# Gate/up products of a decoder trunk: sevens for half of the steps in every second group, and leftovers ordered by priority

## The chip, the core and the metric

The kernel runs on one core of a Trainium2 chip, in one launch. The metric is the device time of an execution in microseconds. Five engines matter: PE (TensorE: matrix products, and its separate weight load PEld), DVE (VectorE), ACT (ScalarE), POOL (GpSimd, almost unused) and SP, whose queue issues the transfers (DMA).

## What is computed

Two layers over 256 tokens of width 2048, all in float32. Layer 0 mixes tokens by causal trailing means, layer 1 by differential attention with eight heads; each is followed by a dense SwiGLU block with 5632 hidden columns. The last step is a normalisation.

```python
for i in range(DEPTH):                       # 2 layers
    hn = rmsnorm(h, norm_mix[i])
    mix = pool_mixer(hn, ...) if i % 2 == 0 else diff_attention(hn, ...)
    h = h + mix
    h = h + swiglu(rmsnorm(h, norm_ffn[i]), w_gate[i], w_up[i], w_down[i])
return rmsnorm(h, final_norm)

def swiglu(h, wg, wu, wd):
    return (jax.nn.silu(h @ wg) * (h @ wu)) @ wd
```

## The kernel before

**Products in two halves.** A float32 operand is split into a high part (`hi`, rounded to the matrix engine's faster float32r type, a cast on ACT) and the rest (`lo`, a subtraction on DVE). A product of two blocks is then three products on PE: high by high, high by low, low by high. Each has 128 x 128 stationary values (activations) and 512 moving columns (weights).

**Groups and steps.** `group()` computes one output of 256 tokens x 1024 columns as 2 x 2 blocks: two blocks of tokens, two blocks of 512 columns. It walks over the contraction in steps of 256 rows; a step takes 1 MB of weights, four blocks of 128 x 512, as one transfer `raw` (`load`). Gate/up has 11 groups a layer (512 gate and 512 up columns each), each of 8 steps. Down has two groups (`o`) for each chunk of the hidden columns; `CHUNKS` says that a chunk is 4, 4 and 3 gate/up groups, so a down group has 8, 8 or 6 steps. The attention layer has four groups for q and k, two for v and two for the output projection, 8 steps each.

**A plain step** makes `whi` and `wlo` of all four blocks (`halves`: 2048 columns on ACT, 2048 on DVE) and issues 4 x 2 x 3 = 24 products into the four PSUM banks C11, C12, C21, C22.

**A step by sevens** computes the same 2 x 2 product of blocks with seven block products in place of eight (the Strassen-Winograd scheme), 7 x 3 = 21 products on PE, into seven banks M1, M2, M6, M7, P5, P3, P4. For that DVE makes four sums of weight blocks (`sums`: one instruction of 1024 columns at L121, two of 512 at L123 and L124), ACT and DVE split these (`thi` at L130, `tlo` at L131, 2048 columns each), and of the raw blocks only three need splitting (1536 columns). The activation pairs of such a step are held in an eight-block form, made once for each pair by `pair()`. Which steps go by sevens is given by `SEVEN` for gate/up, `SEVEN_DOWN`, `SEVEN_QKV` and `SEVEN_O`. With both kinds of step in one group, C11, C12 and C21 share the banks of M2, P3 and P4 (6, 4 and 5), and C22 has bank 7, called X.

**The end of a group.** `combined()` adds the seven results and X into four tiles c11, c12, c21, c22: two copies on ACT, then eight instructions of 512 columns on DVE (L202 to L211). A gate/up group goes on with silu on ACT (L463), a product on DVE (L464), and two calls of `pair()`, which transpose the hidden values on PE into PSUM (L250, a bank of `aux`, which takes banks 0 to 3 in turn), and split them (L254 and L255, or by way of the tile `e`, L263 to L268, where the down step will go by sevens). A down group adds its result to the residual `x_tok` (L487).

**Buffers.** `raw`, `whi` and `wlo` have three buffers each, `tsum`, `thi` and `tlo` one each, the tiles of the combination one each, and each of the eight PSUM banks is a buffer by itself.

**What sets the order.** No order is written out by hand. A scheduler runs through the program at compile time with estimated durations: of the instructions of an engine whose operands and buffers are ready, it takes the one of highest priority, which is the one that stands earliest in the program. The order that it finds is fixed for each engine's queue; on the chip, semaphores hold an instruction until what it needs is done. `tc.high_priority(-n)` moves an instruction's priority back by n places.

Of the kernel before, what the change touches and what calls it, by code (L numbers as in the profile page):

```python
# [38 lines left out]

SEVEN = (2, 4, 6)  # L40
SEVEN_DOWN = (2, 4, 6)
SEVEN_QKV = (4, 6)
SEVEN_O = (6,)


# [7 lines left out]
def trunk_kernel(ctx, tc, x_n, gains, scale_in, final_in, subln, lam_in, band, dist,  # L53
# [18 lines left out]

    turn = {"aux": 0, "of": 4}

    def bank(i, shape=(P, 512)):
        return psum.tile(list(shape), F32, name=f"b{i}", tag=f"b{i}")


# [5 lines left out]
    gain_sb = const.tile([P, 6, NK], F32, name="gain_sb")  # L84
    dist_sb = const.tile([P, 2 * P], F32, name="dist_sb")
    ident = const.tile([P, P], F32, name="ident")
    ones = const.tile([P, P], F32, name="ones")
    nc.vector.memset(ones, 1.0)
    make_identity(nc, ident)

    x_tok = resid.tile([P, 2, D], F32, name="x_tok")
# [8 lines left out]
    def tile_of(xp, k):  # L100
        return xp[k // 2][:, k % 2]

    def f32(ap):
        return ap.bitcast(F32)
# [33 lines left out]
    def group(steps, pool, by_bank=0):  # L138
# [14 lines left out]
        ps = {}  # L153

# [8 lines left out]
        def products(a, seven, w, b, parts):  # L163
            first = b not in ps
            if first:
                ps[b] = bank(b)
            for at, which, block in parts:
                hi, lo = w[which]
                if seven:
                    ah, al = a[:, 0, at], a[:, 1, at]  # L170
                else:
                    k, t = at
                    if a.shape[2] == 8:
                        slot = ((A11, A21), (A12, A22))[k][t]
                        ah, al = a[:, 0, slot], a[:, 1, slot]
                    else:
                        ah, al = (a[:, k, i, t * P:(t + 1) * P] for i in range(2))
                for x, y in ((ah, hi), (ah, lo), (al, hi)):
                    left[b] -= 1
                    nc.tensor.matmul(ps[b], x, y[:, block], start=first, stop=(left[b] == 0))  # L180
                    first = False
# [13 lines left out]
    def combined(ps, pool):  # L195


        if M1 not in ps:
            return [[ps[C11], ps[C12]], [ps[C21], ps[C22]]]
        m1, u2, u3, p5 = (pool.tile([P, 512], F32, name=f"c{i}") for i in ("11", "12", "21", "22"))  # L200
        nc.scalar.copy(m1, ps[M1])
        nc.vector.tensor_tensor(u2, ps[M6], m1, ALU.add)  # L202
        nc.vector.tensor_tensor(m1, ps[M2], m1, ALU.add)  # L203
        nc.vector.tensor_tensor(u3, ps[M7], u2, ALU.add)
        nc.scalar.copy(p5, ps[P5])
        nc.vector.tensor_tensor(u2, p5, u2, ALU.subtract)
        nc.vector.tensor_tensor(p5, p5, u3, ALU.subtract)
        nc.vector.tensor_tensor(u2, ps[P3], u2, ALU.add)
        nc.vector.tensor_tensor(u3, ps[P4], u3, ALU.add)
# [34 lines left out]

    def pair(dst, src, gains, seven):

        ps = aux((P, 2, 2, P))
        for i in range(2):
# [12 lines left out]

        for i, at in ((0, slice(A21, A11 + 1)), (1, slice(A22, A12 + 1, A12 - A22))):
            nc.scalar.activation(e[:, at], ps[:, i], AF.Copy, scale=1.0 if gains is None else gains[i])  # L263
        nc.vector.tensor_tensor(e[:, S1:S3 + 1], e[:, A21:A11 + 1], e[:, A22:A21 + 1], ALU.subtract)
        nc.vector.tensor_tensor(e[:, S2], e[:, S1], e[:, A11], ALU.subtract)
        nc.vector.tensor_tensor(e[:, S4], e[:, A12], e[:, S2], ALU.add)
        nc.scalar.copy(dst[:, 0], e)
        nc.vector.tensor_tensor(dst[:, 1], e, f32(dst[:, 0]), ALU.subtract)  # L268

# [10 lines left out]
    with tc.tile_pool(name="start", bufs=1, reuse_waits="tile") as st:  # L280

        warm = tmp.tile([P, 8], F32, name="warm", bufs=1)
        nc.scalar.activation(warm[:, 0:1], ones[:, 0:1], AF.Sqrt)
        wp = aux()
# [47 lines left out]
        def product(g, some):  # L332

            if some[0] == 0:
                yp[g] = [bank(4 + 2 * (g % 2) + t) for t in range(2)]
                if g >= PLAIN:
# [76 lines left out]
    turn["of"] = 4  # L413
    nc.sync.dma_start(out=dist_sb, in_=dist)

    def finish(cs, ys, final_sb, ss):

        for t in range(2):
            part = tmp.tile([P, 64], F32, name="part", bufs=2)
            nc.vector.tensor_reduce(part[:, 0:1], ss[:, t, 0:2], AX.X, ALU.add)  # L420
# [22 lines left out]
    def ffn(layer, xq, ss, next_op, next_gain):  # L443
# [3 lines left out]
        with tc.tile_pool(name=f"ffn{layer}", bufs=1, reuse_waits="tile") as hp:  # L447
            g0 = 0
            ys = []
            for c, n in enumerate(CHUNKS):  # L450
# [6 lines left out]
                for g in range(g0, g0 + n):  # L457

                    by_seven = SEVEN[-1:] if g == 0 and layer == 0 else SEVEN
                    cs = combined(group([(xq[p], p in by_seven, w_gu[layer][g, p]) for p in range(NP)], hp), hp)  # L460
# [4 lines left out]
                    for i in range(2):  # L465
                        at = 2 * (g - g0) + i
                        ht = hp.tile(pair_shape(at in SEVEN_DOWN), F32R, name="h", tag=f"h{at}")
                        pair(ht, lambda k, t: cs[t][1][:, (2 * i + k) * P:(2 * i + k + 1) * P], None, at in SEVEN_DOWN)
                        hp_tiles.append(ht)
                for o in range(2):  # L470
# [35 lines left out]
    with tc.tile_pool(name="attn", bufs=1, reuse_waits="tile") as ap_, ExitStack() as heads:  # L506
# [3 lines left out]
        qs_col, subln_sb, lam_sb, lp, le, neg_lam, gs = (  # L510
            small[:, a:b] for a, b in ((0, 2), (2, 4), (4, 8), (8, 10), (10, 12), (12, 13), (14, 16)))
        nc.sync.dma_start(out=subln_sb, in_=subln)
        nc.sync.dma_start(out=lam_sb, in_=lam_in)
        r_col = row_scale(ss)
        nc.vector.tensor_scalar(qs_col, r_col, QK_SCALE, None, ALU.mult)

        nc.vector.tensor_tensor(lp, lam_sb[:, 0:2], lam_sb[:, 2:4], ALU.mult)
        l_ps = aux()
# [74 lines left out]
        for g in range(2):  # L593
            cs = scaled(combined(group([(xp[p], p in SEVEN_QKV, w_v[g, p]) for p in range(NP)], op_), op_), (r_col, r_col))
            for h in range(4 * g, 4 * g + 4):
# [11 lines left out]
                for t in range(2):  # L607
                    nc.scalar.activation(on[:, t, :], op[:, t, :], AF.Copy, scale=ro[:, t:t + 1])
                oT[h] = op_.tile(pair_shape(h in SEVEN_O), F32R, name=f"oT{h}")
                pair(oT[h], lambda i, t: on[:, t, i * P:(i + 1) * P], [gs[:, i:i + 1] for i in range(2)], h in SEVEN_O)  # L610
# [98 lines left out]
```

## Time and profile before

| | |
|---|---|
| median of 3 runs (lowest to highest) | 1845.67 us (1845.63 to 1845.7) |
| the profiled execution: time, span of its instructions | 1846.21 us, 1844.4 us |
| PE, weight load, DVE, ACT: busy share of the span | 99%, 81%, 87%, 56% |
| HBM read | 353.36 MB, 193 GB/s over the span |

How to read the rows that follow. An instruction's row gives its start in the span, its duration (both in us), engine, line of the kernel and operation, `out<-in` by the kernel's names, shapes, and a count where several were merged; in square brackets stand the idle time of its engine ahead of it and what ended that. A row of the waits is: who waited, for whom, microseconds in all, times, longest. A row of busy time by stretch gives the stretch, its length, the busy time of PE, PEld, DVE, ACT and POOL with instruction counts, then the granted clock, the DMA share and GB/s. PE's products overlap, so a product's row is longer than its distance to the next.

### The profile page before, as it was taken

To read this page: it belongs to the slowest core of one execution; us is meant where nothing else is said; L and a number is where in the kernel's file an instruction comes from. 1 tells how busy PE (TensorE), PEld (TensorE's weight loads), DVE (VectorE), ACT (ScalarE), POOL (GpSimd) and SP (SyncE) were. 2 spreads that over 40 slices of the span, in tenths; PEclk is the share of its full clock that TensorE was granted. 3 is DMA by queue.
4 is the path that set the end of the run, shared out by engine and by line. 5 is a ranking of instruction groups with operands and counts; after the bars stand their busy time and mean duration, and the time that the engine had idled before them with its cause. 6 is when DMAs were issued, how large, how long until landed. Compare 5 with 4: busy or idle time off the path is not lost.

```text
span 1844.4 us, 20901 instructions
## 1 busy us (share of the span) xinstructions
PE 1829.2 (99%) x8210; PEld 1495.6 (81%) x8210; DVE 1604.2 (87%) x1662; ACT 1038.0 (56%) x1006; POOL 0.7 (0%) x6
## 2 busy tenths in 40 slices
PE   9999999999999999999999999999999999999998
PEld 6788888888888888888888888788888888888886
DVE  6889998898989899988888678998989899998986
ACT  6555555555554556665566655555555555545553
POOL 0000000000000000000000000000000000000000
PEclk9999999999999999999999999999999999999999
DMA  7555555655555555555454454555555555565552
GB/s 273 183 201 187 193 210 194 210 196 194 203 198 204 202 186 183 208 180 171 173 177 164 160 188 176 205 203 187 204 205 204 188 201 183 206 227 204 206 186 111
DMA packets 50642, 356.80 MB, mean 193 GB/s; under 512 B 6000, under 2 KB 6128, under 8 KB 8048
## 3 DMA queue, kind: packets, MB, share of 16 engines
q1 hardware_dynamic: 49824, 353.85, 54.4%
q10 hardware_dynamic: 720, 1.62, 0.2%
q8 instruction: 64, 1.05, 0.2%
q14 instruction: 34, 0.28, 0.0%
HBM read 353.36 MB, written 2.10 MB: 193 GB/s over the span
## 4 chain that ended last, share of the span: by engine, by line
PE 95%; DVE 2%; ACT 1%; issue 1%; DMA 1%; SPq 0%; DVEq 0%; ACTq 0%
PE b L180 90%; PE b L250 2%; PE b L342 1%; DVE wlo L116 1%; PE b L554 1%; PE b L345 1%; PE b L584 0%; DMA w<-pool_w 0%; DMA raw<-w_gu 0%; DVE tlo L131 0%; ACT whi L115 0%; DVE tsum L121 0%; PE b L600 0%; PE b L598 0%; PE b L599 0%
## 5 line engine op out<-in xcount | busy, mean ns | idle before, releaser
L115 ACT CAST whi<-raw 128x1536 fp32r<-128x1536 f32 (+1 forms) x330 | 585.2, 1774 | 585.4 <-PE b L180 499.6
L180 PE MATMUL b<-whi,xp 128*128 128x512 f32 x2824 | 908.8, 392 | 1.2 <-DVE c L203 1.0
L116 DVE TENSOR_TENSOR wlo<-raw,whi 128x1536 fp32r<-128x1536 f32 (+1 forms) x330 | 697.3, 2113 | 193.1 <-ACT whi L115 192.9
L180 PEld LDWEIGHTS b<-whi,xp 128*128 128x128 f32 x2824 | 528.3, 188 | 110.1 <-DVE c L203 1.5
L180 PE MATMUL b<-wlo,xp 128*128 128x512 f32 x1412 | 551.8, 391 | 1.6 <-DVE wlo L116 1.6
L180 PE MATMUL b<-whi,h 128*128 128x512 f32 x1108 | 354.5, 390 | 0.0
L180 PEld LDWEIGHTS b<-wlo,xp 128*128 128x128 f32 x1412 | 265.3, 188 | 55.5 <-DVE wlo L116 1.9
L131 DVE TENSOR_TENSOR tlo<-tsum,thi 128x2048 fp32r<-128x2048 f32 x108 | 246.7, 2285 | 3.9 <-ACT thi L130 3.9
L180 PEld LDWEIGHTS b<-whi,h 128*128 128x128 f32 x1108 | 207.5, 188 | 43.1
L180 PE MATMUL b<-wlo,h 128*128 128x512 f32 x554 | 215.8, 389 | 0.0
L130 ACT CAST thi<-tsum 128x2048 fp32r<-128x2048 f32 x108 | 206.3, 1910 | 13.7 <-DVE tsum L124 13.6
L180 PE MATMUL b<-thi,xp 128*128 128x512 f32 x608 | 211.8, 390 | 0.0
L121 DVE TENSOR_TENSOR tsum<-raw 128x1024 f32<-128x1024 f32 x108 | 131.8, 1220 | 2.3 <-DMA raw<-w_v 0.6
L180 PEld LDWEIGHTS b<-thi,xp 128*128 128x128 f32 x608 | 113.9, 188 | 24.0 <-ACT thi L130 0.9
L180 PEld LDWEIGHTS b<-wlo,h 128*128 128x128 f32 x554 | 104.0, 188 | 21.3
L180 PE MATMUL b<-tlo,xp 128*128 128x512 f32 x304 | 119.5, 393 | 0.0
L180 PE MATMUL b<-thi,h 128*128 128x512 f32 x240 | 83.7, 389 | 0.0
L124 DVE TENSOR_TENSOR tsum<-tsum,raw 128x512 f32<-128x512 f32 x108 | 74.3, 688 | 2.3
L123 DVE TENSOR_TENSOR tsum<-tsum,raw 128x512 f32<-128x512 f32 x108 | 73.9, 684 | 0.6
L180 PE MATMUL b<-whi,oT 128*128 128x512 f32 x236 | 74.4, 392 | 0.0
L180 PEld LDWEIGHTS b<-tlo,xp 128*128 128x128 f32 x304 | 57.0, 188 | 16.1 <-DVE tlo L131 4.4
L180 PEld LDWEIGHTS b<-thi,h 128*128 128x128 f32 x240 | 45.1, 188 | 9.2
(147 smaller groups left out, 1192.5 us busy)
## 6 DMA issues: line engine op xcount, KB each, us to landing
raw<-w_gu SPq DMA_DIRECT2D x176, 1024.0 KB, 4.9
raw<-w_down SPq DMA_DIRECT2D x88, 1024.0 KB, 4.8
raw<-w_qk SPq DMA_DIRECT2D x32, 1024.0 KB, 4.9
raw<-w_v SPq DMA_DIRECT2D x16, 1024.0 KB, 4.8
raw<-w_o SPq DMA_DIRECT2D x16, 1024.0 KB, 4.8
raw<-pool_w SPq DMA_DIRECT2D x2, 1024.0 KB, 13.8
x_tok<-x_n SPq DMA_DIRECT2D x2, 768.0 KB, 9.0
w<-pool_w SPq DMA_DIRECT2D x2, 512.0 KB, 6.6
```

The source lines that it names most:

```text
L115: nc.scalar.copy(hi[:, lo_block:], raw[:, lo_block:])
L116: nc.vector.tensor_tensor(lo[:, lo_block:], raw[:, lo_block:], f32(hi[:, lo_block:]), ALU.subtract)
L121: nc.vector.tensor_tensor(t[:, T1:T3 + 1], raw[:, B11:B22 + 1], raw[:, B12:B12 + 1].broadcast_to([P, 2, 512]), ALU.add)
L123: nc.vector.tensor_tensor(t[:, T2], t[:, T1], raw[:, B22], ALU.add)
L124: nc.vector.tensor_tensor(t[:, T4], t[:, T2], raw[:, B21], ALU.add)
L130: nc.scalar.copy(hi, t)
L131: nc.vector.tensor_tensor(lo, t, f32(hi), ALU.subtract)
L180: nc.tensor.matmul(ps[b], x, y[:, block], start=first, stop=(left[b] == 0))
L250: nc.tensor.transpose(ps[:, i, 1 - t if seven else t], src(i, t), ident)
L342: nc.tensor.matmul(yp[g][t], a[:, rows], w[:, at], start=(at == 0), stop=(at == 3))
L345: nc.tensor.matmul(yp[g][t], u, v[:, at], start=(at == 0 and j == 0), stop=(at == 3 and j == 2))
L554: nc.tensor.matmul(sc[:, :nk], qk[:, 0, c, qb * P:(qb + 1) * P], qk[:, 1, c, :nk], start=True, stop=True)
```

## The change

1. `SEVEN` becomes (0, 2, 4, 6). In a chunk, the gate/up groups at even places (first, third) take `SEVEN[1:]`, steps 2, 4, 6 as before; those at odd places take all four. The very first group keeps step 6 alone. Attention's output projection and the start now prepare x's pair 0 in the eight-block form.
2. In a step by sevens the three products of raw blocks come first (M1, M2, P3), then P5, M7, M6 and P4; in a group's step 0, P3 comes later.
3. Banks 4 and 5 are one tile of two banks. The combination writes one tile `c` of 4 x 512 columns, and does its two subtractions, and its two additions from banks 4 and 5, in one instruction of 1024 columns each.
4. `pair()` of a gate/up group transposes into bank X, both calls one behind the other, in place of the banks of `aux`.
5. The `e` instructions of such a pair, and the residual additions behind a down group that isn't a layer's last (now two of 1024 columns), are moved back by 150 places of priority.
6. Memory: `ones`, `part` and `dist_sb` become short-lived, `dist` is loaded at the start of attention, and four of the attention outputs `oT` take the place of x's pairs.

```diff
-SEVEN = (2, 4, 6)
+SEVEN = (0, 2, 4, 6)
+BEHIND = 150
...
+    def two_banks():
+        both = psum.tile([P, 2, 512], F32, name="b45", tag="b45")
+        return [both[:, i] for i in range(2)], both
+    def behind(n):
+        return tc.high_priority(-n) if n else nullcontext()
...
-                plan.append([(M1, [(A11, 0, B11)]), (M2, [(A12, 0, B21)]), (M6, [(S2, 1, T2)]), (M7, [(S3, 1, T3)]),
-                             (P5, [(S1, 1, T1)]), (P3, [(S4, 0, B22)]), (P4, [(A22, 1, T4)])])
+                raw = [(M1, [(A11, 0, B11)]), (M2, [(A12, 0, B21)]), (P3, [(S4, 0, B22)])]
+                summed = [(P5, [(S1, 1, T1)]), (M7, [(S3, 1, T3)]), (M6, [(S2, 1, T2)]), (P4, [(A22, 1, T4)])]
+                late = 3 if plan else 2
+                plan.append(raw[:late] + summed[:3] + raw[late:] + summed[3:])
...
-        m1, u2, u3, p5 = (pool.tile([P, 512], F32, name=f"c{i}") for i in ("11", "12", "21", "22"))
+        c = latest["c"] = pool.tile([P, 4, 512], F32, name="c")
+        m1, u2, u3, p5 = (c[:, i] for i in range(4))
...
-        nc.vector.tensor_tensor(u2, p5, u2, ALU.subtract)
-        nc.vector.tensor_tensor(p5, p5, u3, ALU.subtract)
-        nc.vector.tensor_tensor(u2, ps[P3], u2, ALU.add)
-        nc.vector.tensor_tensor(u3, ps[P4], u3, ALU.add)
+        nc.vector.tensor_tensor(c[:, 1:4:2], c[:, 3:4].broadcast_to([P, 2, 512]), c[:, 1:3], ALU.subtract)
+        nc.vector.tensor_tensor(c[:, 1:3], ps["both"], c[:, 1:3], ALU.add)
...
-    def pair(dst, src, gains, seven):
-        ps = aux((P, 2, 2, P))
+    def pair(dst, src, gains, seven, at=None):
+        ps = aux((P, 2, 2, P)) if at is None else bank(at, (P, 2, 2, P))
...
+        with behind(BEHIND if at is not None else 0):
+            (the three instructions on e, and the split of e into dst)
...
-                    by_seven = SEVEN[-1:] if g == 0 and layer == 0 else SEVEN
+                    by_seven = (SEVEN if (g - g0) % 2 else SEVEN[1:]) if g or layer else SEVEN[-1:]
...
-                        pair(ht, lambda k, t: ..., None, at in SEVEN_DOWN)
+                        pair(ht, lambda k, t: ..., None, at in SEVEN_DOWN, X)
...
+                    if not last:
+                        with behind(BEHIND):
+                            for t in range(2):
+                                to = x_tok[:, t, o * 1024:(o + 1) * 1024]
+                                nc.vector.tensor_tensor(to, latest["c"][:, 2 * t:2 * t + 2].rearrange("p b n -> p (b n)"),
+                                                        to, ALU.add)
+                        continue
```

More of the change, by code (lines that the diff above doesn't have):

```diff
@@ L1 @@
 import math
-from contextlib import ExitStack
+from contextlib import ExitStack, nullcontext
 import concourse.bass as bass
@@ L163, in products @@
         def products(a, seven, w, b, parts):
-            first = b not in ps
-            if first:
+            first = b not in opened
+            opened.add(b)
+            if first and b in (P3, P4) and b not in ps:
+                (ps[P3], ps[P4]), ps["both"] = two_banks()
+            elif first and b not in ps:
                 ps[b] = bank(b)
@@ L260, in pair @@
         e = tmp.tile([P, 8, P], F32, name="e", bufs=1)
[L262 to L268, printed above, removed]
+        for i, to in ((0, slice(A21, A11 + 1)), (1, slice(A22, A12 + 1, A12 - A22))):
+            nc.scalar.activation(e[:, to], ps[:, i], AF.Copy, scale=1.0 if gains is None else gains[i])
+        with behind(BEHIND if at is not None else 0):
+            nc.vector.tensor_tensor(e[:, S1:S3 + 1], e[:, A21:A11 + 1], e[:, A22:A21 + 1], ALU.subtract)
+            nc.vector.tensor_tensor(e[:, S2], e[:, S1], e[:, A11], ALU.subtract)
+            nc.vector.tensor_tensor(e[:, S4], e[:, A12], e[:, S2], ALU.add)
+            nc.scalar.copy(dst[:, 0], e)
+            nc.vector.tensor_tensor(dst[:, 1], e, f32(dst[:, 0]), ALU.subtract)
     def transposed(xp, j, gain, seven=()):
@@ L280, in trunk_kernel @@
     with tc.tile_pool(name="start", bufs=1, reuse_waits="tile") as st:
+        ones = st.tile([P, P], F32, name="ones")
+        nc.vector.memset(ones, 1.0)
         warm = tmp.tile([P, 8], F32, name="warm", bufs=1)
+        make_identity(nc, ident)
         nc.scalar.activation(warm[:, 0:1], ones[:, 0:1], AF.Sqrt)
@@ L334, in product @@
             if some[0] == 0:
-                yp[g] = [bank(4 + 2 * (g % 2) + t) for t in range(2)]
+                yp[g] = [bank(6 + t) for t in range(2)] if g % 2 else two_banks()[0]
                 if g >= PLAIN:
@@ L413, in trunk_kernel @@
     turn["of"] = 4
-    nc.sync.dma_start(out=dist_sb, in_=dist)
     def finish(cs, ys, final_sb, ss):
         for t in range(2):
-            part = tmp.tile([P, 64], F32, name="part", bufs=2)
+            part = tmp.tile([P, 8], F32, name="warm", bufs=1) if t == 0 else \
+                tmp.tile([P, 2, 4], F32, name="ss").rearrange("p a b -> p (a b)")
             nc.vector.tensor_reduce(part[:, 0:1], ss[:, t, 0:2], AX.X, ALU.add)
@@ L467, in ffn @@
                         ht = hp.tile(pair_shape(at in SEVEN_DOWN), F32R, name="h", tag=f"h{at}")
[L468 removed]
+                        pair(ht, lambda k, t: cs[t][1][:, (2 * i + k) * P:(2 * i + k + 1) * P], None, at in SEVEN_DOWN, X)
                         hp_tiles.append(ht)
@@ L511, in trunk_kernel @@
             small[:, a:b] for a, b in ((0, 2), (2, 4), (4, 8), (8, 10), (10, 12), (12, 13), (14, 16)))
+        dist_sb = hq.tile([P, 2 * P], F32, name="dist_sb")
+        nc.sync.dma_start(out=dist_sb, in_=dist)
         nc.sync.dma_start(out=subln_sb, in_=subln)
@@ L515, in trunk_kernel @@
         nc.vector.tensor_scalar(qs_col, r_col, QK_SCALE, None, ALU.mult)
+        ones = hq.tile([P, P], F32, name="ones")
+        nc.vector.memset(ones, 1.0)
         nc.vector.tensor_tensor(lp, lam_sb[:, 0:2], lam_sb[:, 2:4], ALU.mult)
@@ L608, in trunk_kernel @@
                     nc.scalar.activation(on[:, t, :], op[:, t, :], AF.Copy, scale=ro[:, t:t + 1])
-                oT[h] = op_.tile(pair_shape(h in SEVEN_O), F32R, name=f"oT{h}")
+                if h < 4:
+                    oT[h] = op_.tile(pair_shape(h in SEVEN_O), F32R, name=f"oT{h}")
+                else:
+                    oT[h] = resid.tile(pair_shape(h in SEVEN_O), F32R, name="xp", tag=f"xp{h}")
                 pair(oT[h], lambda i, t: on[:, t, i * P:(i + 1) * P], [gs[:, i:i + 1] for i in range(2)], h in SEVEN_O)
```

7 lines of the change are left out of this document (2 added, 5 removed).

## The prediction

> **What bounds the kernel now.** I read the page first: shares of the engines, clock, chain.
>
> ```profile
> span 1844.4 us, 20901 instructions
> PE 1829.2 (99%) x8210; PEld 1495.6 (81%) x8210; DVE 1604.2 (87%) x1662; ACT 1038.0 (56%) x1006; POOL 0.7 (0%) x6
> PEclk9999999999999999999999999999999999999999
> PE 95%; DVE 2%; ACT 1%; issue 1%; DMA 1%; SPq 0%; DVEq 0%; ACTq 0%
> ```
>
> TensorE is on the chain for 95% of the span at full granted clock. A busy PE alone proves little, so I looked at its rhythm in the chain in order of time, which merges unbroken runs of products (L180):
>
> ```profile
> 57.74 38.16 PE b L180 x168
> 225.09 124.34 PE b L180 x547
> ```
>
> 38.16 / 168 and 124.34 / 547 both give 0.227 us for a product of 512 columns: that is its price on the path. The waits say what interrupts this rhythm, and what VectorE waits for:
>
> ```profile
> ACT whi L115 <- PE b L180: 499.6, 224, 4.7
> DVE wlo L116 <- ACT whi L115: 192.9, 146, 4.2
> PEld b L180 <- DVE tlo L131: 6.9, 17, 0.4
> PE b L180 <- DVE wlo L116: 1.6, 1, 1.6
> PE b L180 <- DVE c L203: 1.0, 1, 1.0
> ```
>
> PE waits almost never. ACT waits 500 us for PE to give back a weight buffer, DVE 193 us for ACT: the preparation runs ahead until its three buffers are full. So PE is the bound, and DVE the engine nearest to becoming one. How near shows in the busy time by stretch of one gate/up group (169 to 212) and of the second down group of a chunk (254.7 to 296.2); columns: us, then PE, PEld, DVE, ACT, POOL:
>
> ```profile
> 169.20:212.00 42.80, 42.80 (x193) 35.06 (x192) 38.86 (x35) 24.24 (x21) 0.00 (x0) 1.00 0.55 198
> 254.70:296.20 41.50, 41.50 (x184) 34.36 (x183) 37.56 (x32) 20.66 (x15) 0.00 (x0) 1.00 0.57 203
> ```
>
> In a gate/up group DVE has 42.8 - 38.9 = 3.9 us to spare. The sum hangs on that number.
>
> **The change, part by part.** The base is the profiled execution, 1846.21 us (span 1844.42 and 1.79 around it); the median of the three runs, 1845.67, is 0.54 below it and takes the same differences.
>
> *Products removed.* A plain step issues 4 x 2 x 3 = 24 products, one by sevens 7 x 3 = 21. Step 0 goes by sevens in each group at an odd place of its chunk, "G" below: 2 + 2 + 1 a layer, 10 in all. The other groups ("F") keep steps 2, 4, 6, and the first group of all keeps step 6. So 10 x 3 = 30 products go: 30 x 0.227 = **-6.8 us**, if PE stays the bound. The Trainium skill, page "TensorE: Matmul & The Clock Gate", section "Back-to-back issue gap", puts a sustained product of 512 columns at about 131 ns; by that the term would be -3.9, but the two runs above disagree.
>
> *VectorE work added.* What an instruction occupies is the distance to the next start, a little under its duration. DVE where one group ends and the next begins (start, duration, line):
>
> ```profile
> 172.19 1.21 DVE L121 TENSOR_TENSOR tsum<-raw 128x1024 f32<-128x1024 f32 x1
> 173.33 0.68 DVE L204 TENSOR_TENSOR c<-b,c 128x512 f32<-128x512 f32 x1
> 175.12 2.28 DVE L116 TENSOR_TENSOR wlo<-raw,whi 128x2048 fp32r<-128x2048 f32 x1
> 177.33 0.68 DVE L207 TENSOR_TENSOR c<-c,c 128x512 f32<-128x512 f32 x1
> 177.93 0.68 DVE L208 TENSOR_TENSOR c<-b,c 128x512 f32<-128x512 f32 x1
> 178.53 0.68 DVE L209 TENSOR_TENSOR c<-b,c 128x512 f32<-128x512 f32 x1
> 181.65 1.75 DVE L116 TENSOR_TENSOR wlo<-raw,whi 128x1536 fp32r<-128x1536 f32 x1
> 183.32 0.41 DVE L264 TENSOR_TENSOR e<-e 128x256 f32<-128x256 f32 x1
> ```
>
> So: 2048 columns 2.21, 1536 1.67, 1024 1.14, 512 0.60. A plain step costs DVE 2.21; one by sevens 1.14 + 0.60 + 0.60 (tsum) + 2.21 (tlo) + 1.67 = 6.22, 4.0 more. Merging two subtractions and two additions of the combination into 1024-column instructions saves 2 x 0.06. A group G then asks DVE for 38.9 + 4.0 - 0.1 = 42.8 us against PE's 42.8 - 0.7 = 42.1: 0.7 too much. With the F group beside it, 38.9 - 0.1 in 42.8, the pair asks 81.6 of 84.9. It fits if 0.7 us may slip across a group's border. Priced at nothing, with the F groups' 3.9 us as cover; without cover it costs 10 x 0.7 = 7. ACT gets 1.4 us more in a G group, and has 18 to spare. DMAs stay as many; SP only gets the 128 KB for dist later, ahead of an attention that first wants it a group (40 us) after.
>
> *Order of the seven products.* Today P3 comes sixth; now the three products of raw blocks come first (two in step 0 of a group). The first use of thi/tlo moves back by three products, 0.68 us. That meets the 17 waits for tlo above; on PE one of them looks so:
>
> ```profile
> 147.90 0.84 PE L180 MATMUL b<-thi,xp 128*128 128x512 f32 x3
> 148.97 0.50 PE L180 MATMUL b<-tlo,xp 128*128 128x512 f32 x1
> 149.31 0.39 PE L180 MATMUL b<-thi,xp 128*128 128x512 f32 x1
> ```
>
> The third of the x3 starts at about 148.58, so the next was due at 148.81: 0.16 late, and 0.34 - 0.23 = 0.11 behind it, 0.27 us a time. These waits stand at step 2 of groups that follow a gate/up group. Twelve of those groups are F or down groups and get the 0.68: -12 x 0.27 = **-3.2 us** (ends: 0, and -4.6 for all 17).
>
> *A G group's first step.* Its tlo needs thi's single buffer, which PE gives back at the end of step 6 of the group before, 24 products or 5.4 us ahead of the border; it is due six products (1.4 us) behind the border: 6.8 us. ACT needs 1.9 for thi, tlo 2.2, and the combination of the old group asks for DVE at the same time (M6, M2, M7 at 0.60, subtraction 1.14, PSUM addition 1.14, X 0.60). The first four, 2.94 us, fit beside thi; P3/P4 finish only 1.4 us ahead of the border. Walked through, tlo ends about 2 us early, step 2's about 1.4. Bounds for each border: 0, and 1.8 (rival below). I take today's nearest wait, 0.27: 10 x 0.27 = **+2.7 us**.
>
> *Start.* x's first pair of blocks is now prepared in the eight-block form, while DVE is full and PE waits for it:
>
> ```profile
> 38.59 0.88 DVE L243 SCALAR_TENSOR_TENSOR xp<-b,gain_sb,xp 128x256 fp32r<-128x256 f32 x2
> 44.80 0.43 DVE L264 TENSOR_TENSOR e<-e 128x256 f32<-128x256 f32 x1
> 45.74 0.29 DVE L265 TENSOR_TENSOR e<-e 128x128 f32<-128x128 f32 x1
> 46.34 0.28 DVE L266 TENSOR_TENSOR e<-e 128x128 f32<-128x128 f32 x1
> 48.25 1.21 DVE L268 TENSOR_TENSOR xp<-e,xp 128x1024 fp32r<-128x1024 f32 x1
> 54.71 0.50 PE L180 MATMUL b<-wlo,xp 128*128 128x512 f32 x1 [1.65 <-DVE wlo L116]
> ```
>
> 2.21 - 0.88 = 1.3 by durations, 1.1 by starts: **+1.1 us** (0 to 1.9). The same pair in layer 1 is made under the second w_o group.
>
> *Transposes of h* go through bank X, one pair behind the other, where today both pairs run together:
>
> ```profile
> 220.17 0.39 PE L180 MATMUL b<-whi,h 128*128 128x512 f32 x1
> ...
> 223.59 0.38 PE L250 MATMUL b<-ident,c 128*128 128x128 f32 x2
> 223.72 0.48 PE L180 MATMUL b<-whi,h 128*128 128x512 f32 x1
> 224.04 0.39 PE L180 MATMUL b<-wlo,h 128*128 128x512 f32 x1
> 224.27 0.82 PE L250 MATMUL b<-ident,c 128*128 128x128 f32 x6
> ...
> 224.79 0.66 ACT L263 ACTIVATE e<-b 128x256 f32<-128x256 f32 x2 [2.10 <-PE b L250]
> 225.34 0.59 ACT L254 CAST h<-b 128x512 fp32r<-128x512 f32 x1
> ```
>
> More changes between transposes and products follow; each costs PE about 0.09 (224.04 - 223.72 = 0.32 to the next start instead of 0.23). Half a change for 22 groups: **+1.0** (0 to 2).
>
> *At no price:* banks 4 and 5 come free together, about 0.6 us later for bank 4 (it is the second bank of a plain first step, due 1.4 us behind the border; today L208 and L209 end just about there, so the spare is a few tenths); h's e-chain moves back in priority, into DVE's spare moments (h is read a down group later); the residual additions too, and since c is now one buffer, the next group's first copy into c on ACT, with the weight casts behind it, waits for them: they are 2 x 1.14 us in the course of a group with 3.9 to spare (41.5 - 37.6 in the down group above); ones, part, dist, oT moved in memory.
>
> Sum: -6.8 - 3.2 + 2.7 + 1.1 + 1.0 = -5.2: 1846.2 to 1841.0 for a profiled run, **1840.5** for the median.
>
> **The rivals.**
>
> *It cancels out* (within 0.2%, 3.7 us, about what a measurement of this kernel can tell). The mechanism works, but tlo or wlo come 0.4 to 1.1 us late at the ten F-to-G borders. For it: the 17 waits of today arise behind two plain steps, 6.4 us of DVE relief which a G group lacks. Against: h's e-chain, which stood ahead of that tlo, is now put back (as long as that of x above, 1.9 by starts). -7.9 (the sum without the border's 2.7) + (4 to 11) gives 1842 to 1849.
>
> *DVE becomes the bound at the border* (slower). In a G group DVE is asked for 42.8 in 42.1 us, and the 4.0 come first, where the combination's burst falls. If nothing else moves, step 0 or 2 is late by 0.27 + 4.0 - 0.68 (order) - 1.9 (h put back) = 1.7 to 1.8 us, ten times: -7.9 + 18 = +10, 1856. It decides from 0.8 us a border. For it: DVE idles only 3.9 us in a whole group. Against: 193 us of DVE waiting for full buffers. The Trainium skill, page "Perfetto Trace Analysis", section "Identifying the Most-Contended Engine", would judge TensorE by weight-load busy time, here 81%, under DVE's 87%, which makes DVE the engine to relieve and speaks for this rival; the chain's 95% on PE speaks against it.
>
> *Bank X holds up the next group* (slower). A plain first step needs X for its last 6 products, 18 x 0.227 + 0.9 (the eight transposes) = 5.0 us behind the border. With pairs in succession X comes free later: in the rows of h above the border is at 220.1 and the first pair's copies end at 225.4; four transposes 0.45, hi 0.59 and lo 0.60 make it 227.0, 6.9 behind. At best DVE's share is 1 us earlier in other groups: 1 to 2 us at 12 borders that a plain step follows, 1850 to 1862. It happens only if PE's queue holds these six products ahead of the next step's. Against: the x2 and x6 above stand in the middle of the next group's products, so PE's order already bends to what is ready.
>
> **How the numbers follow.** Forecast 0.60 (1834.5 to 1842: from -6.8 - 4.6 with no new cost, to the 0.2% line); cancelled 0.22; DVE bound 0.11; bank X 0.07. The range 1834.5 to 1850 leaves out the two slow cases. Faster 0.60, same 0.22, slower 0.18.
>
> **What would show it.** L180 products down by 30; the wait for tlo gone from step 2 of F and down groups; DVE 90% or more in G groups with PE's idle time there under 0.5 us; DVE 1 us later at 45 to 58 us. Wrong if a PE wait for tlo, wlo or c of a microsecond recurs at every second group, or if X's products run late with PE idle.

## The result: slower by 1.5%, outside the predicted range

The changed kernel takes 1873.7 us (median of 4 runs, 1871.06 to 1875.62) beside 1845.68 for the kernel before on the same chip: a ratio of 1.0151, 95% interval 1.0133 to 1.0168. The prediction was 1840.5, its range ended at 1850. The profiled execution of the changed kernel is the fastest of its four, 1871.06 us with a span of 1869.3; its span is 24.9 us longer than that of before.

The page after, the same lines as before:

```profile
span 1869.3 us, 20771 instructions
PE 1833.8 (98%) x8180; PEld 1484.3 (79%) x8180; DVE 1635.0 (87%) x1609; ACT 1043.5 (56%) x1018; POOL 0.7 (0%) x6
PEclk9999999999999999999999999999999999999999
PE 70%; DVE 16%; ACT 5%; issue 5%; DMA 4%; SPq 0%; ACTq 0%; DVEq 0%
```

PE executes 8180 products in place of 8210: the 30 are gone. But the chain, 95% PE before, is PE for 70% only, and DVE, ACT and even DMA stand on it. 87% busy for DVE is what it was before. The chain no longer follows one busy engine; it zigzags between engines that wait for one another. PE idles 1869.3 - 1833.8 = 35.5 us; before it was 15.2.

Two of the waits before that count here, `thi` for `tsum` and `tlo` for `thi`:

```profile
ACT thi L130 <- DVE tsum L124: 13.6, 29, 4.0
DVE tlo L131 <- ACT thi L130: 3.9, 3, 2.0
```

The waits after (products are L190, `whi`/`wlo` L120/L121, the last part of `tsum` L129, `thi`/`tlo` L135/L136, the two-bank addition of the combination L218):

```profile
ACT thi L135 <- DVE tsum L129: 170.6, 66, 5.0
DVE wlo L121 <- ACT whi L120: 99.1, 92, 4.2
DVE tlo L136 <- ACT thi L135: 91.2, 52, 2.1
PEld b L190 <- DVE c L218: 14.4, 15, 1.5
PEld b L190 <- DVE tlo L136: 14.2, 22, 1.6
PEld b L190 <- ACT thi L135: 10.2, 28, 0.6
PE b L190 <- DVE c L218: 8.6, 12, 1.1
PE b L190 <- DVE tlo L136: 7.1, 12, 1.2
```

Before, DVE waited 193 us for `whi`: it had run ahead and found the buffers full. Now that is 99 us, and in its place ACT waits 171 us for `tsum` and DVE 91 us for `thi`. (ACT also waits 39.0 us for gate/up weights to land, 4.4 before. `raw` has three buffers, and a late sum holds one of them; that this is the reason was not tested apart.) Below stand the stalls of PE: on `tlo`, and on the two-bank addition at a group's border. (A wait of PEld lies partly beside a product that still runs; the PE rows are what was lost for certain.)

Summing the distances from each product to the next in the trace, PE spent 21.3 us beyond 0.227 a product before and 53.4 after, 32 more. Some 31 stalls of a quarter of a microsecond or more make up most of it: 23.8 us, where 4 came to 2.3 before. Another 3.1 us are products that stand right behind a transpose or another small product (149 that cost 14.3 us, 118 and 11.2 before); the rest is spread over shorter delays. Less the 6.8 us of products that are gone, that is 25.3, nearly the whole of the 24.9.

Two stretches of the two FFN layers show who is short of time (busy time by stretch: us, PE, PEld, DVE, ACT, POOL; clock, DMA share, GB/s). Before, then after:

```profile
68.00:248.00 180.00, 180.00 (x807) 147.89 (x806) 160.17 (x142) 99.52 (x77) 0.00 (x0) 1.00 0.55 196
```

```profile
68.00:248.00 180.00, 176.77 (x787) 143.46 (x786) 163.61 (x139) 100.30 (x79) 0.00 (x0) 1.00 0.53 190
1195.00:1375.00 180.00, 177.07 (x785) 143.53 (x785) 167.44 (x140) 97.19 (x75) 0.00 (x0) 1.00 0.55 199
```

After, no engine is full over the stretch. PE idles 3.2 of 180 us, and DVE idles 16.4 us in the same stretch: the time goes to engines that wait for one another, not to the work of one engine.

How it comes about is seen in the first G group (ACT, then DVE; start, duration):

```profile
112.44 1.91 ACT L135 CAST thi<-tsum 128x2048 fp32r<-128x2048 f32 x1 [4.68 <-DVE tsum L129]
...
123.12 1.91 ACT L135 CAST thi<-tsum 128x2048 fp32r<-128x2048 f32 x1 [5.00 <-DVE tsum L129]
```

```profile
114.38 2.29 DVE L136 TENSOR_TENSOR tlo<-tsum,thi 128x2048 fp32r<-128x2048 f32 x1 [2.05 <-ACT thi L135]
116.59 1.75 DVE L121 TENSOR_TENSOR wlo<-raw,whi 128x1536 fp32r<-128x1536 f32 x1
118.26 1.22 DVE L126 TENSOR_TENSOR tsum<-raw 128x1024 f32<-128x1024 f32 x1
119.40 2.28 DVE L121 TENSOR_TENSOR wlo<-raw,whi 128x2048 fp32r<-128x2048 f32 x1
121.60 0.68 DVE L128 TENSOR_TENSOR tsum<-tsum,raw 128x512 f32<-128x512 f32 x1
122.32 0.69 DVE L129 TENSOR_TENSOR tsum<-tsum,raw 128x512 f32<-128x512 f32 x1
125.07 2.29 DVE L136 TENSOR_TENSOR tlo<-tsum,thi 128x2048 fp32r<-128x2048 f32 x1 [2.06 <-ACT thi L135]
...
136.44 1.21 DVE L218 TENSOR_TENSOR c<-b,c 128x1024 f32<-128x1024 f32 x1
```

Read it as a ring. `tsum` has one buffer, which `tlo` still reads. So the next `tsum` comes only behind `tlo` (here behind a `wlo` as well); it spans 118.26 to 123.01, because a `wlo` is fitted in between. Then ACT makes `thi` until 125.03, with DVE idle for 2.06 us, then comes `tlo`. From `tlo` to `tlo` it is 125.07 - 114.38 = 10.7 us, and in it sum, cast and subtraction each wait for the one before. PE runs one step by sevens and one plain step in 45 x 0.227 = 10.2. The ring is no faster than PE: a sum that is late once stays late for the rest of the group. In the second G group (177.6 to 221.3) `tlo` ends at 183.9, 196.3, 207.0 and 216.1, each 2.8 to 4.7 us behind the moment at which, by the number of products done, the planned order would use it. PE then takes products of the next plain step first, the summed products slip towards the end of the group, and the combination starts late.

In the kernel before, a turn was shorter:

```profile
189.37 2.28 DVE L131 TENSOR_TENSOR tlo<-tsum,thi 128x2048 fp32r<-128x2048 f32 x1
...
195.82 2.28 DVE L116 TENSOR_TENSOR wlo<-raw,whi 128x2048 fp32r<-128x2048 f32 x1
198.02 2.29 DVE L131 TENSOR_TENSOR tlo<-tsum,thi 128x2048 fp32r<-128x2048 f32 x1
```

From `tlo` to `tlo` it took 8.65 us, with the same instructions. There the long `wlo` ran beside `thi`; after, it is put inside the sum, and DVE has nothing to do beside `thi`. So the length of a turn depends on where the `wlo` is put; against 10.2 it left 1.5 us to catch up in this turn before, and none in the turn after.

PE pays at the border (PE, after; the first ends a wait for the L218 above):

```profile
137.71 0.50 PE L190 MATMUL b<-whi,xp 128*128 128x512 f32 x1 [0.62 <-DVE c L218]
...
226.41 0.50 PE L190 MATMUL b<-whi,h 128*128 128x512 f32 x1 [1.05 <-DVE c L218]
```

At the first of these borders DVE is full for a while, and it is so as well in g3, a kernel described below that has the same instructions at the border but a shorter ring. Busy time around it, the changed kernel and then g3:

```profile
129.50:140.00 10.50, 9.88 (x44) 7.77 (x43) 10.50 (x13) 3.04 (x4) 0.00 (x0) 1.00 0.55 201
```

```profile
126.00:136.00 10.00, 10.00 (x46) 8.29 (x45) 10.00 (x10) 5.57 (x6) 0.00 (x0) 1.00 0.59 211
```

Both show DVE without a gap, but only in the first does PE stop. The difference is when the burst begins: g3 starts the two-bank addition at 134.45, the changed kernel at 136.44.

### The profile page after: what moved, and what is told of

It is laid out like the page before. It is cut to its first block, busy times and chain, and to the rows that moved or that the text cites. A ratio compares the mean times of both kernels' runs of the same rounds, so it can differ in the third digit from the quotient of the medians.

```text
span 1869.3 us, 20771 instructions
## 1 busy us (share of the span) xinstructions
PE 1833.8 (98%) x8180; PEld 1484.3 (79%) x8180; DVE 1635.0 (87%) x1609; ACT 1043.5 (56%) x1018; POOL 0.7 (0%) x6
## 3 DMA queue, kind: packets, MB, share of 16 engines
q8 instruction: 64, 1.05, 0.2%
## 4 chain that ended last, share of the span: by engine, by line
PE 70%; DVE 16%; ACT 5%; issue 5%; DMA 4%; SPq 0%; ACTq 0%; DVEq 0%
PE b L190 66%; DVE wlo L121 6%; ACT whi L120 3%; ACT thi L135 2%; DVE tlo L136 2%; DMA raw<-w_gu 2%; DMA raw<-w_down 2%; PE b L259 2%; DVE tsum L126 1%; DVE c L217 1%; DVE c L218 1%; PE b L578 1%; DVE c L213 1%; DVE c L215 1%; DVE tsum L129 1%
## 5 line engine op out<-in xcount | busy, mean ns | idle before, releaser
L190 PE MATMUL b<-whi,xp 128*128 128x512 f32 x2832 | 907.5, 393 | 3.7 <-DVE c L218 3.7
L120 ACT CAST whi<-raw 128x1536 fp32r<-128x1536 f32 (+1 forms) x330 | 577.6, 1760 | 437.1 <-PE b L190 352.9
L121 DVE TENSOR_TENSOR wlo<-raw,whi 128x1536 fp32r<-128x1536 f32 (+1 forms) x330 | 689.4, 2095 | 99.9 <-ACT whi L120 99.1
L190 PEld LDWEIGHTS b<-whi,xp 128*128 128x128 f32 x2832 | 530.0, 188 | 118.0 <-DVE c L218 6.9
L190 PE MATMUL b<-wlo,xp 128*128 128x512 f32 x1416 | 555.1, 392 | 0.2 <-DVE wlo L121 0.2
L190 PE MATMUL b<-whi,h 128*128 128x512 f32 x1108 | 353.5, 392 | 5.9 <-DVE c L218 4.8
L136 DVE TENSOR_TENSOR tlo<-tsum,thi 128x2048 fp32r<-128x2048 f32 x118 | 270.0, 2288 | 92.0 <-ACT thi L135 91.2
L135 ACT CAST thi<-tsum 128x2048 fp32r<-128x2048 f32 x118 | 225.5, 1911 | 188.8 <-DVE tsum L129 170.6
L190 PEld LDWEIGHTS b<-wlo,xp 128*128 128x128 f32 x1416 | 266.2, 188 | 53.9 <-DVE wlo L121 0.6
L190 PEld LDWEIGHTS b<-whi,h 128*128 128x128 f32 x1108 | 207.7, 188 | 53.3 <-DVE c L218 7.5
L190 PE MATMUL b<-thi,xp 128*128 128x512 f32 x704 | 236.6, 394 | 0.5 <-ACT thi L135 0.2
L190 PE MATMUL b<-wlo,h 128*128 128x512 f32 x554 | 215.9, 390 | 0.0
L190 PEld LDWEIGHTS b<-thi,xp 128*128 128x128 f32 x704 | 130.1, 188 | 34.9 <-ACT thi L135 10.2
L126 DVE TENSOR_TENSOR tsum<-raw 128x1024 f32<-128x1024 f32 x118 | 143.6, 1217 | 2.3 <-DMA raw<-w_v 1.6
L190 PE MATMUL b<-tlo,xp 128*128 128x512 f32 x352 | 139.1, 395 | 6.4 <-DVE tlo L136 6.4
L190 PEld LDWEIGHTS b<-wlo,h 128*128 128x128 f32 x554 | 104.1, 188 | 20.8
L190 PEld LDWEIGHTS b<-tlo,xp 128*128 128x128 f32 x352 | 66.1, 188 | 25.7 <-DVE tlo L136 12.3
L129 DVE TENSOR_TENSOR tsum<-tsum,raw 128x512 f32<-128x512 f32 x118 | 80.7, 684 | 0.7
L128 DVE TENSOR_TENSOR tsum<-tsum,raw 128x512 f32<-128x512 f32 x118 | 80.6, 683 | 0.4
L190 PE MATMUL b<-thi,h 128*128 128x512 f32 x240 | 78.9, 389 | 0.0
L476 ACT ACTIVATE c<-c,r_tok 128x512 f32<-128x512 f32 x44 | 31.8, 723 | 48.4 <-DVE c L214 30.6
L190 PEld LDWEIGHTS b<-thi,h 128*128 128x128 f32 x240 | 45.1, 188 | 9.3
```

The lines of the kernel that those rows point to most:

```text
L120: nc.scalar.copy(hi[:, lo_block:], raw[:, lo_block:])
L121: nc.vector.tensor_tensor(lo[:, lo_block:], raw[:, lo_block:], f32(hi[:, lo_block:]), ALU.subtract)
L126: nc.vector.tensor_tensor(t[:, T1:T3 + 1], raw[:, B11:B22 + 1], raw[:, B12:B12 + 1].broadcast_to([P, 2, 512]), ALU.add)
L128: nc.vector.tensor_tensor(t[:, T2], t[:, T1], raw[:, B22], ALU.add)
L129: nc.vector.tensor_tensor(t[:, T4], t[:, T2], raw[:, B21], ALU.add)
L135: nc.scalar.copy(hi, t)
```

## The experiments

The texts on record name theories by letters. S is that the extra step by sevens costs where its chain and the combination meet, at a group's border; C is a form of it, the ring just described: single buffers of `tsum`, `thi` and `tlo` keep the sums late. D is that DVE has too much work in a G group. P is that the moved priorities delay something. M is that the two-bank tile costs by itself. All times are medians; "before" ran beside them at 1845.67 to 1845.91.

### Which part of the change costs

**e1**: the changed kernel without the extra sevens.

```diff
-SEVEN = (0, 2, 4, 6)
+SEVEN = (2, 4, 6)
-by_seven = (SEVEN if (g - g0) % 2 else SEVEN[1:]) if g or layer else SEVEN[-1:]
+by_seven = SEVEN if g or layer else SEVEN[-1:]
```

> The changed kernel with steps 2, 4, 6 alone by sevens in every gate/up group, as before; order of products, two-bank tile, bank X, priorities and memory stay changed. Theory S (the extra step by sevens at a group's border costs: its tsum, thi, tlo chain and the combination meet there): the stalls go, and what is left is the gain of the new order of products: 1840 to 1846. Theory M (the two-bank addition and the transposes in bank X cost by themselves): they stay here, 1852 to 1862, with waits for the two-bank addition of some 10 us in all on PE.

Measured: 1847.22 us, ratio 1.0007 (0.9998 to 1.0017), 1.2 above the range of S and far under that of M. All the rest of the change together costs nothing that can be told from zero, and gains nothing. (ACT waits 82.7 us for `tsum` in this kernel too, and 13.6 in the one before. Such a wait is a sign of the ring and not its price.)

**e2**: the changed kernel with banks 4 and 5 as buffers of their own.

```diff
-        nc.vector.tensor_tensor(c[:, 1:3], ps["both"], c[:, 1:3], ALU.add)
+        nc.vector.tensor_tensor(u2, ps[P3], u2, ALU.add)
+        nc.vector.tensor_tensor(u3, ps[P4], u3, ALU.add)
```

> The changed kernel with banks 4 and 5 as two buffers again and two additions of 512 columns in place of one of 1024. In the changed kernel PE waited 8.6 us (weight load 14.4) for the two-bank addition, and that wait is 1.2 us at four borders into a down group. Theory M: these waits go, 1873 - 9 to 14 = 1859 to 1864. Theory S: the addition is late because DVE is late there; one bank comes free 0.5 us earlier, the waits shrink by a few us at most: 1867 to 1872.

Measured: 1856.9 us, ratio 1.0061 (1.0046 to 1.0076): 16.8 us less than the changed kernel, more than either text allowed. With one tile PE waits for the end of the 1.21 us addition; apart, each bank comes back behind an instruction of 0.68. PE's own waits for these additions fall from 8.6 us to 1.2, and its stalls of a quarter of a microsecond or more from 23.8 to 10.4.

**e3**: nothing is moved back in priority.

```diff
-BEHIND = 150
+BEHIND = 0
```

> The changed kernel with nothing moved back in priority (0 in place of 150 places). Theory P (the residual additions, moved back, come when the next gate/up group's prepared weights are due; the changed kernel loses about 3 us at each border from the second down group into a gate/up group): that border's loss goes, four times 3 us, 1858 to 1863. Theories S and M: h's e-chain returns to the border and adds up to 1.9 us at ten of them: 1875 to 1890.

Measured: 1874.73 us, ratio 1.0158 (1.0142 to 1.0173), which overlaps the changed kernel's. P falls; that h's instructions cost at the border where they are not moved back, as the text says under S and M, is not seen either.

**e6**: the kernel before with the extra sevens and the memory moves that make room for them (point 6 of the change), and nothing else.

```diff
-SEVEN = (2, 4, 6)
+SEVEN = (0, 2, 4, 6)
-by_seven = SEVEN[-1:] if g == 0 and layer == 0 else SEVEN
+by_seven = (SEVEN if (g - g0) % 2 else SEVEN[1:]) if g or layer else SEVEN[-1:]
```

> The kernel before with the extra step by sevens in ten groups and the memory moves that it needs, and nothing else: old order of products, separate banks, transposes in banks 0 to 3, no priorities moved. Theory S: as slow as the changed kernel or slower, since nothing helps at the border, 1868 to 1890. Theory M: only the border's own cost is left, 1838 to 1850.

Measured: 1858.58 us, ratio 1.0074 (1.0059 to 1.0089). The part that was to save 6.8 us costs 12.8 by itself, so it brings nearly 20 us of new waiting. This lies between the ranges of S and M: neither has the size right as it was put. Its waits (`thi` L126, `tsum` L120, the combination at L199 and L204, with banks apart):

```profile
ACT thi L126 <- DVE tsum L120: 60.6, 46, 4.5
PEld b L176 <- ACT thi L126: 10.7, 23, 1.7
PEld b L176 <- DVE c L199: 10.1, 10, 1.0
PEld b L176 <- DVE c L204: 7.7, 10, 0.8
```

The last two come ten times: one for each G group, at its end.

### Ring, or too much work

**e7 and e8** give the instructions of the sums (`tsum`, `thi`, `tlo`) 40 places more priority: e7 on e2, e8 on the kernel before.

```diff
+                with tc.high_priority(40):
+                    t = sums(pool, raw)
```

> The kernel with split banks (1857), and the sums of weight blocks and their split (tsum, thi, tlo) raised by 40 places of priority, over the preparation of the plain step ahead of them. In its groups with four steps by sevens tlo comes 1 to 5 us after its products are due, and stays late: tsum has one buffer, can't start until the last tlo is written, and takes 4.7 us there in place of 2.4, since plain steps' wlo stand between. Theory C (this ring of single buffers, tsum - thi - tlo, takes as long as the two steps it serves and so never catches up): raised, it takes 2.3 us less, tlo is on time again, 1843 to 1850. Theory D (DVE has too much to do there): what one chain gains, wlo loses: 1853 to 1862.

> The kernel before with the same 40 places for the sums and their split. There the chain isn't late but for 0.27 us at step 2 of 17 groups: theory C: 0 to 4 us faster, 1841 to 1846. Theory D: no change or slower, 1845 to 1850.

Measured: e7 1864.2 us (1.0098, 1.0083 to 1.0113), 7.3 worse than e2; e8 1841.33 us (0.9977, 0.9968 to 0.9986), 4.3 better than before. e8 is as C has it. e7 is a miss: it lies above the ranges of both C and D. One reading is that what is put behind the sums comes late instead (the waits of PE for `wlo` rose from 3.7 to 5.2 us), while in the kernel before the ring has slack and an earlier start pays. That wasn't tested further.

**c1 and d1** are the pair that decides. Memory has no room for a second `tsum`, so c1, made from e2, makes some:

```diff
-SEVEN_DOWN = (2, 4, 6)
+SEVEN_DOWN = (4, 6)
-        sq = tmp.tile([P, 512], F32, name="sq", bufs=1)
+        sq = tmp.tile([P, 512], F32, name="sq", tag="e", bufs=1)
... (and the same for the two other `sq`)
```

d1 is c1 with one word more (and the same word for the last step's `y`, which uses that buffer):

```diff
-        t = pool.tile([P, 4, 512], F32, name="tsum")
+        t = pool.tile([P, 4, 512], F32, name="tsum", bufs=2)
```

> Control for the next one: the kernel with split banks, with steps 4 and 6 alone by sevens in the down groups (11 groups x 3 products x 0.227 = 7.5 us more on PE) and sq in e's buffer, which frees memory. Both theories: 1857 + 7.5 = 1862 to 1867, with the same waits in the gate/up groups.

> The control with two buffers for tsum, nothing else changed: the sums of the next step by sevens needn't wait for the last tlo. Theory C: the ring is cut, the waits of the gate/up groups go, 8 to 14 us less than the control: 1850 to 1857. Theory D: DVE has the same work, 0 to 3 us less: 1860 to 1866.

Measured: c1 1864.6 us (1.0106, 1.009 to 1.0121); d1 1843.44 us (0.9989, 0.9979 to 0.9998). One more buffer is worth 21 us, more than the 8 to 14 that C forecast. The pages' shares, c1 first and then d1:

```profile
PE 1837.9 (99%) x8213; PEld 1493.5 (80%) x8213; DVE 1596.0 (86%) x1588; ACT 1025.6 (55%) x997; POOL 0.7 (0%) x6
```

```profile
PE 1827.9 (99%) x8213; PEld 1494.8 (81%) x8213; DVE 1590.4 (86%) x1588; ACT 1027.8 (56%) x997; POOL 0.7 (0%) x6
```

Both give DVE 1588 instructions and 86%; the work is the same, only when it may begin, and with it the order that the scheduler finds, differs. D can't explain that. The ring's own wait shows it, again c1 and then d1:

```profile
ACT thi L134 <- DVE tsum L128: 114.5, 42, 5.0
```

```profile
ACT thi L134 <- DVE tsum L128: 62.6, 25, 3.9
```

**f2** keeps down's sevens: e2 with each step's four sums in two tiles of half the size, each with its own `thi` and `tlo`; the first tile has two buffers. `sq` is in the buffer of `e` here too.

```diff
-        t = pool.tile([P, 4, 512], F32, name="tsum")
+        t = pool.tile([P, 2, 512], F32, name="tsa", bufs=2)
+        u = pool.tile([P, 2, 512], F32, name="tsb")
```

> The changed kernel with banks 4 and 5 apart, and each step's four sums in two tiles of half the size, each with its own thi and tlo; all other sums by sevens kept, down's too. Theory C: a sum of two halves releases its buffers earlier, the ring turns in about half the time, and the stalls before products on tlo go: 1834 to 1843. Against it: more and shorter instructions on ScalarE and VectorE; if these count for more than the ring, 1846 to 1857.

Measured: 1834.93 us, ratio 0.9941 (0.9928 to 0.9953). It is the fastest kernel of this study, 11.0 us under before. Its stretch, and its products' largest waits for VectorE that are left:

```profile
68.00:248.00 180.00, 180.00 (x810) 148.53 (x809) 171.31 (x165) 105.87 (x96) 0.00 (x0) 1.00 0.55 194
```

```profile
PEld b L191 <- DVE wlo L120: 1.8, 2, 0.9
PEld b L191 <- DVE c L219: 1.1, 4, 0.5
```

In 180 us DVE does 171.3 us of work, 7.7 more than in the changed kernel, and PE never stops. This is the plainest line against D.

### Do the removed products count, once the ring is cut

Pairs with and without the extra sevens (the edit of e1): d1 and **f4**; f2 and **g4**; and in the order of the kernel before **g1** (e6 with half sums) and **g2**. **f1** is the kernel before with the memory moves, `sq` in the buffer of `e`, and two buffers for `tsum` (d1's line). The text on record says that f1 has the extra sevens as well; that is wrong, it keeps steps 2, 4 and 6, so f1 says at most what the ring cost in the kernel before, and g1 does what f1 was said to do.

> The kernel before with the sums by sevens in steps 2, 4 and 6 of a G group as well (the edit that cost +12.8 us by itself), and one more thing: two buffers for tsum, so that the next sum can be written before thi and tlo of the last have been. Theory C (the ring of single buffers tsum, thi, tlo keeps the sums late): the 12.8 us go, and the 30 products saved (6.8 us) remain at least in part: 1838 to 1846. Theory D (VectorE has too much to do in a G group): still 1855 or more.

> The kernel with banks apart, two buffers for tsum and down's sevens in steps 4 and 6, which took 1843.4 us, but gate and up with sevens in steps 2, 4 and 6 of every group: 30 products more (6.8 us by 0.227 us each). If the ring was all that ate the saving: 1848 to 1852. If the saving is eaten elsewhere too: 1842 to 1846.

> The kernel with banks apart and half sums, 1834.9 us, without the extra sevens: 30 products more at 0.227 us: 1840 to 1843. If the saving is still partly eaten: 1835 to 1839.

> The kernel before with the extra sums by sevens (the edit that cost +12.8 us by itself) and each step's sums in two tiles of half the size, with their own thi and tlo; nothing else of the change but its memory moves. Theory C: with the ring cut the 12.8 us go and 30 products (6.8 us) are won: 1830 to 1837. If half sums rescue only the reordered kernel, or VectorE has too much to do in a G group: 1842 to 1855.

> The same with gate and up by sevens in steps 2, 4 and 6 alone, as before: half sums without the extra sevens. Two buffers for tsum gave 1839.0 us on the kernel before; halves do the same with four more short instructions a step: 1837 to 1843, and 6.8 us above the kernel with half sums and the extra sevens if each removed product counts in full.

| kernel | us | ratio (95%) | with extra sevens | difference |
|---|---|---|---|---|
| f1 | 1838.97 | 0.9963 (0.9951 to 0.9976) | | |
| f4 | 1850.22 | 1.0024 (1.0015 to 1.0033) | d1 1843.44 | -6.8 |
| g4 | 1839.85 | 0.9968 (0.9957 to 0.9979) | f2 1834.93 | -4.9 |
| g2 | 1837.8 | 0.9958 (0.9945 to 0.997) | g1 1836.75 | -1.0 |

The range of f1's text held for another kernel than the one it describes, so it counts for nothing; f1's own result is that the kernel before gets 6.9 us faster with no step added. Not all of that is the ring's: the memory moves were not run alone, and 1.8 us of it are there by the end of the first group (its last product, the 189th, starts at 90.23 in place of 92.06), where only one step goes by sevens. g4, at 1839.85, falls between its text's two ranges.

In the order of the changed kernel the extra sevens bring 6.8 us with a second `tsum` and 4.9 with half sums. In the order of before (g1) they bring 1.0, within the uncertainty of the two ratios: g1 is inside the range of its text, but the difference of 6.8 that g2's text gives is missed, and C alone does not explain that. No stall of a quarter of a microsecond recurs there at G's borders; what is left are single waits at the start of each layer and behind two groups. Three of g1 that g2 lacks or has smaller:

```profile
53.78 0.50 PE L180 MATMUL b<-wlo,xp 128*128 128x512 f32 x1 [0.52 <-DVE wlo L112]
93.34 0.44 PE L250 MATMUL b<-ident,c 128*128 128x128 f32 x2 [0.92 <-DVE c L467]
1178.43 0.50 PE L180 MATMUL b<-wlo,xp 128*128 128x512 f32 x1 [1.24 <-DVE wlo L112]
```

By distances these and one of 0.6 us at 1428 come to 3.3 us more than in g2, and the first product starts 1.3 us later. The remaining 1 to 2 us of g1 weren't traced.

### Does the two-bank addition cost by itself

**f3** is the changed kernel with its two-bank tile, two buffers for `tsum`, and down's sevens as in c1; its partner with banks apart is d1. **g3** is the changed kernel with the half sums of f2 (its diff above), which is its partner.

> The changed kernel with its two-bank addition kept, two buffers for tsum, and down's sums by sevens in steps 4 and 6 alone (to make room). Theory C: the two-bank addition cost 16.8 us only because VectorE reached it late; with the ring cut it costs little: 1843 to 1849. Rival M (TensorE waits for the whole of a two-bank addition whenever it comes): 1855 or more.

> The changed kernel, its two-bank addition kept, with half sums as its only edit (and sq in the buffer of e). Theory C: of the 16.8 us that the two-bank tile cost, most go once VectorE reaches the addition in time; the pair with two buffers for tsum kept 4.1 us: 1836 to 1841. Rival M (the two-bank tile costs by itself): 1846 or more.

Measured: f3 1847.5 us (1.0008, 0.9999 to 1.0017), 4.1 above d1; g3 1837.66 us (0.9958, 0.9946 to 0.9971), 2.7 above f2. Of 16.8 us most were an effect of the late sums, as C has it; M keeps a rest of 2.7 to 4.1 us, whose place wasn't settled. g3 is the changed kernel with the ring cut and little else, 36 us faster than it.

One comparison more is in these numbers. The kernel before with the same half sums, g2, takes 1837.8 us and g3 1837.66. Once both have the shorter ring, the whole change gains nothing that can be told from zero; with banks apart as well (f2) it gains 2.9.

## Why the prediction was wrong, by its own steps

By the runs the 28.0 us come apart like this: the rest of the change without the extra sevens +1.5 (e1), the products removed -6.8, and the waiting that the extra sevens bring +33.3.

*Products removed, -6.8.* The price was right: 0.227 us a product stands in every unbroken run of products. Its condition, "if PE stays the bound", was not met: PE had 35.5 us of idle time. Where the ring is cut, the 30 products brought 6.8, 4.9 and 1.0 us, the dearer start (below) included.

*VectorE work added.* The amounts were right, and so was the conclusion that they fit: f2 carries them with PE full. But "it fits if 0.7 us may slip across a group's border" asked only whether the busy time fits. That is the step that failed. Nobody may work ahead through a single buffer: the 3.9 us to spare in an F group can't be used for the sums of the G group behind it while `tlo` still reads `tsum`. With one more buffer for `tsum` and the same work, 21 us of waiting went (c1 and d1).

*A G group's first step, +2.7.* This is the term in which the failure shows. It was walked through for steps 0 and 2 alone, by the moment at which `thi`'s buffer comes back, and each border was then taken by itself. `tsum`'s buffer and what follows in steps 4 and 6 were left out. The number to compare was the turn of the ring, `tsum` 2.3, `thi` 1.9, `tlo` 2.2 and what DVE fits in between, against 10.2 us for a pair of steps. The trace of before showed a turn that took 8.65, so even that sum would have warned only of a margin of 1.5 us, not of the order in which it vanishes. Measured, the extra sevens cost 12.8 + 6.8 = 19.6 us in e6 and, between e1 and the changed kernel, 26.5 + 6.8 = 33.3, where 2.7 to 18 stood between forecast and rival.

*Order of products, -3.2.* The waits for `tlo` at step 2 do go in e1, as said (0.2 us are left of 6.9), and e1 is not faster. Two things stand against it in e1's trace: the next term, and a first group whose last product starts 1.2 us later (93.30 against 92.06), behind a wait of 2.39 us for `wlo` at 54.60 and products at half rate after it.

*Transposes, +1.0 (0 to 2).* Eleven more changes at 0.09 were forecast. In g2 and g4, which have the same work in the order of before and in that of the change, 116 and 149 products stand behind a change, and they cost 11.2 and 14.5 us. So the number of changes was too low by a factor of three. g4 is 2.1 us above g2 in all; as the order of products, the priorities and the merged subtraction differ too, the net size of this term stays open.

*Start, +1.1 (0 to 1.9).* The first product of the gate/up groups begins 1.9 us later (before, then after):

```profile
43.84 0.39 PE L180 MATMUL b<-whi,xp 128*128 128x512 f32 x1
```

```profile
45.78 0.40 PE L190 MATMUL b<-whi,xp 128*128 128x512 f32 x1
```

That isn't the price, for by the 49th product it is made up (60.33 before, 59.93 after). The pairs with and without the extra sevens show the term: the last product of the first group starts 1.4 us later in d1 than in f4, 0.6 later in f2 than in g4 and 1.4 later in g1 than in g2. The forecast of 1.1 was good.

*At no price.* For banks 4 and 5 the prediction named the cover, "a few tenths" of spare at the border, and did not charge its loss. With sums that are late by 3 to 5 us the cover is gone in every second group: 16.8 us (e2). For the priorities, no price was the right one (e3).

*The rivals.* "DVE becomes the bound at the border" had the place right: the waits for L218 stand there, DVE is full for the 10 us around it, and the rival was charged 1856. Its mechanism, too much work, does not hold: g3 has the same burst at the border without a stall, and f2 does more DVE work than the changed kernel in the same 180 us. The Trainium skill, page "Perfetto Trace Analysis", section "Identifying the Most-Contended Engine", had been drawn on for it; the pair c1 and d1, with nearly the same busy shares and 21 us apart, shows that no comparison of busy shares, this rule or mine, could have told. "Bank X" did not decide: PEld waited 4.6 us in all for the copies out of it (L272). "It cancels out" names a result, 1842 to 1849, in which the change comes out with a second `tsum` buffer (d1, f3), but not by the mechanism given for it, and d1 and f3 give up a step by sevens in each down group as well. With half sums it comes out at 1837.66 (g3), inside the range of the forecast itself; but there the kernel before would take 1837.8.

*What would show it wrong* was named rightly: a PE wait for `tlo` or `c` at every second group. It was half a microsecond to a microsecond, as in the rows above (0.62 and 1.05).

## What to carry to other kernels

Before work is added to an engine that has time to spare, look for the buffers that its chain passes through: if a result is made, split and subtracted in single buffers over two engines, add up one turn of that ring, with what the scheduler fits in between, and compare it with the period of the engine it feeds. Here the same instructions made a turn of 8.65 or of 10.7 us by their order alone, beside a period of 10.2, so a margin of that size is none. Two helper engines that wait for each other, while the engine they feed waits too, are the sign of a ring; here a second buffer or tiles of half the size cured it, with the work left as it was. Merging two instructions or two banks is free only as long as nobody is waiting for the first half. And before a gain is booked for the change, run the old kernel with the same cure: here it took all of the gain.

## What the runs showed of the hardware

After a wait of 2.45 us the products of e2 ran for about 3 us at half the rate, 0.43 us from one to the next, and so again after two waits in a row, 1.52 and 1.14 us, at 1222 us; so did those of e1 after a wait of 2.39 (e2, PE; then its stretch, where the granted clock stands behind POOL):

```profile
55.60 0.57 PE L187 MATMUL b<-wlo,xp 128*128 128x512 f32 x1 [2.45 <-DVE wlo L120]
...
56.82 0.63 PE L187 MATMUL b<-wlo,xp 128*128 128x512 f32 x1
57.24 0.63 PE L187 MATMUL b<-whi,xp 128*128 128x512 f32 x1
57.67 0.63 PE L187 MATMUL b<-wlo,xp 128*128 128x512 f32 x1
```

```profile
54.00:58.00 4.00, 2.40 (x6) 1.95 (x7) 4.00 (x5) 2.39 (x6) 0.00 (x0) 0.74 0.31 86
```

The wait of 1.65 us in the kernel before, and the one of 1.24 in g1, were followed by full rate. The Trainium skill, page "TensorE: Matmul & The Clock Gate", section "What's actually happening", tells of such a gate, with half rate after an idle window of about 3.4 us; here a wait of 2.45 us was enough. The 40 slices of e2's profile page don't show it: all stand at 9. Seven products at 0.43 in place of 0.23 are 1.4 us lost behind a stall of 2.45.
